# Fifteen loads of 1 to 15 partitions behind the 62nd tile of a nanmax

## The chip, the cores and the metric

The kernel runs on one core of one Trainium2 chip. The metric is the device time of one execution in microseconds (us). Four of the core's engines matter here: ScalarE (ACT), VectorE (DVE) and GpSimd (POOL), which compute, and SyncE (SP), which issues the DMAs. The transfers themselves run on 16 DMA engines.

## The reference

```
batch, seq, dim = 32, 2048, 2048
x = np.random.randn(batch, seq, dim).astype(np.float32)
x[np.random.rand(batch, seq, dim) < 0.1] = np.nan
np.nanmax(x, axis=-1).astype(np.float32)
```

It is a maximum over the last axis that passes over NaN: 65536 rows of 2048 float32 values go in (537 MB), 65536 values come out (0.26 MB).

## The kernel before

The rows are split over 128 partitions. A partition holds 512 rows, and a tile is a stretch of these, given in quarters of a row (`Q` = 512 values, 2 KB per partition). `TILES` lists the tiles in order; each has three lists in quarters: its loads, its pieces for the cleaning of NaN, and its reductions. Tile 1 has one load of 4 quarters. Tiles 2 to 62 have one load of 28 quarters each, which is 57344 bytes per partition and 7168 KB in all. From tile 63 on a tile has several loads, which get smaller towards the end (down to 1 quarter). `GROUPS` cuts the list into six groups; each has its own stretch of the input (`xg`) and of the output (`og`). The 62nd tile is the second of the fifth group.

There are three tile buffers `xt` (`BUFS`), so the load of tile 63 goes into the buffer of tile 60 and has to wait until DVE has reduced that one. A load (L316) is issued by SP, in program order. It waits for its buffer (`before`) and for the earlier load on its own lane: there are 14 lanes (`LANES`), one semaphore each, taken in turn.

For each piece ACT makes a key of the upper 16 bits of every value (L222, `kt<-xt`), and POOL turns the key back (L232, `xt<-kt`), so that NaN becomes a value that loses every comparison; a piece that is written with a minus sign is turned back by ACT instead. DVE takes the maximum of the cleaned rows (L239) into `acc`. At the end of some groups a short instruction corrects `acc` for rows without numbers (L245 on DVE; L260 and L274 on POOL for the fifth group).

The class `Order` keeps the order by hand. Its `add` issues an instruction, gives it the semaphore waits that its engine hasn't yet seen, directly or through another event, and lets it raise the semaphore of its lane. Only the last wait stands on the instruction; the others become instructions of their own in front of it (L158). Six stores of `acc` (L461), one for each group, come last on SP. Each waits for the event that makes its part of `acc` ready, and a last wait of SP holds the end of the program until they have landed.

Of the kernel before, what the change touches and what calls it, by code (L numbers as in the profile page):

```python
# [62 lines left out]
LEAD = 128  # L63

LANES = 14

# [104 lines left out]
def kernel(  # L173
# [15 lines left out]
    nc = tc.nc  # L189
    P = nc.NUM_PARTITIONS  # L190
    f32, i32 = mybir.dt.float32, mybir.dt.int32
# [14 lines left out]
    sing = ctx.enter_context(tc.tile_pool(name="sing", bufs=1))  # L206
# [4 lines left out]
    kts = [sing.tile([P, KEYS], u16, name=f"kt{i}") for i in range(NKEYS)]  # L211
    accs = sing.tile([P, sum(rows)], f32, name="acc")
    late = sing.tile([P, rows[LATE]], i32, name="late")

    with tc.tile_critical():  # L215
        order = Order(nc)
# [11 lines left out]
        def pool(deps, pair=None, **kw):  # L228
            return order.add(
                "pool",  # L230
                nc.gpsimd,
                lambda: nc.gpsimd.tensor_scalar(**kw),  # L232
                deps,
                lane=pair,
                joint=pair is not None,
            )

        def dve(deps, do, **kw):
            return order.add("dve", nc.vector, lambda: do(**kw), deps)  # L239

        def find(deps, acc):
            return order.add(
                "dve",
                nc.vector,
                lambda: nc.vector.scalar_tensor_tensor(  # L245
                    out=acc,
                    in0=acc,
                    scalar=LEAST,
                    in1=acc,
                    op0=ALU.is_ge,  # L250
                    op1=ALU.mult,
                ),
                deps,
            )
# [36 lines left out]
        number = 0  # L291
        lanes = [[] for _ in range(LANES)]
        turn = 0
        stores = []
        ready = []
        flagged = 0
        r0 = 0
        for gi, (s, g) in enumerate(zip(rows, GROUPS)):
            xg = xr[r0 : r0 + P * s].rearrange("(p s) d -> p (s d)", p=P)
# [5 lines left out]
            for loads, pieces, reds in g:  # L305
# [5 lines left out]
                for c in loads:  # L311
                    c *= Q
                    e = order.add(
                        "sp",
                        nc.sync,
                        lambda: nc.sync.dma_start(  # L316
                            out=xt[:, at : at + c], in_=xg[:, base + at : base + at + c]
                        ),
                        before + lanes[turn],
                        lane=f"load{turn}",  # L320
                        step=16,
                    )
                    lanes[turn] = [e]
                    turn = (turn + 1) % LANES
                    landed.append((at, at + c, e))
                    at += c
                clean = []
                after = []
                at = done = 0
# [24 lines left out]
                def name(i):  # L354
                    return f"pair{number}_{pairs[i][0]}" if i in pairs else None
# [15 lines left out]
                for parts in pieces:  # L371
# [4 lines left out]
                    if used + c > KEYS:  # L376
# [9 lines left out]
                        out=kts[key][:, used : used + c],  # L386
                        in_=xt[:, at : at + c].bitcast(i16)[:, 1::2],
# [6 lines left out]
                    for c in parts:  # L394
# [9 lines left out]
                        else:  # L404
                            e = pool(
                                [e_key],
                                name(piece),
                                out=to,
                                in0=kp,
                                scalar1=-1.0,  # L410
                                scalar2=float(TOP),
                                op0=ALU.mult,
                                op1=ALU.add,
# [4 lines left out]
                        while reds and done + reds[0] <= min([at] + open_):  # L418
                            n = reds.pop(0)
# [7 lines left out]
                            else:  # L427
                                m = max(n // D, 1)
                                to = acc[:, row : row + m]
                            e = dve(  # L430
                                [e for a, b, e in clean if b > lo and a < done] + part,
                                nc.vector.tensor_reduce,
                                out=to,
                                in_=xt[:, lo:done]
                                .bitcast(f32)
                                .rearrange("p (c d) -> p c d", c=m),
                                axis=mybir.AxisListType.X,
                                op=ALU.max,
# [13 lines left out]
            else:  # L452
                e = find(after, accs[:, lo:flagged])
# [3 lines left out]
        for (og, bits), e in zip(stores, ready):  # L457
            last = order.add(
                "sp",
                nc.sync,  # L460
                lambda: nc.sync.dma_start(out=og, in_=bits),  # L461
                [e],
                lane="store",
                step=16,
            )
# [38 lines left out]
```

## Time and profile before

| | |
|---|---|
| median of 3 runs | 1252.53 us (1252.52 to 1252.58) |
| profiled execution | 1252.48 us, of which the span is 1250.7 |
| POOL busy | 1168.5 us (93%), 242 instructions |
| DVE busy | 1111.4 us (89%), 179 instructions |
| ACT busy | 965.6 us (77%), 273 instructions |
| read from memory, written | 536.87 MB, 0.26 MB, 429 GB/s over the span |
| DMA packets | 15991, 2544 of them under 512 bytes |
| ACT's idle time before L222, ended by a load | 257.9 us in 69 waits |
| SP's waits for DVE before a load | 1155.4 us in 71 waits |
| tile loads of 7168 KB, issue to landing | 22.6 us (median of 61) |

The span runs from the first to the last recorded instruction; the time of an execution also holds what lies around it. In the profile, L316 is a line of the kernel, and "kt<-xt" says what an operation writes and reads, with the buffer numbers left out. A share of busy time is a mean over the whole span: which engine holds up the others has to be read from the waits at each place. DMA packets are the pieces that one DMA engine moves at a time: a load of 128 partitions is 128 packets, eight for each of the 16 engines, and on each engine a packet of 4 bytes follows, which raises the semaphore.

### The profile page before, as it was taken

What the parts mean: (1) busy time and instruction counts of PE and PEld (TensorE: products, weight loads), DVE (VectorE), ACT (ScalarE), POOL (GpSimd) and SP (SyncE); (2) the same over time, 40 slices, a digit from 0 to 9 for tenths busy, and PEclk for the clock granted to TensorE, in tenths of its full rate; (3) what the DMA queues carried; (4) which work ended last, traced back from release to release, by engine and by line L of the source; (5) the groups of instructions that cost most, each with busy time, mean ns of one, the idle gap of its engine ahead of it and who ended that gap; (6) DMA issues with size and microseconds to landing.
All of it is one profiled execution on the core that took longest, in us unless ns stands there. A gap on an engine that the chain in (4) does not pass through costs nothing.

```text
span 1250.7 us, 891 instructions
## 1 busy us (share of the span) xinstructions
DVE 1111.4 (89%) x179; ACT 965.6 (77%) x273; POOL 1168.5 (93%) x242
## 2 busy tenths in 40 slices
DVE  0888989888889888898988888998888899999999
ACT  3777887778777877788777877777777778999997
POOL 2999989998999899998999899999999999989998
DMA  9999999999999999999999999999999999999997
GB/s 415 440 418 433 440 440 438 413 440 440 440 433 418 440 440 438 429 424 440 440 436 424 431 440 438 436 424 433 440 438 435 422 436 436 425 434 429 431 428 301
DMA packets 15991, 537.20 MB, mean 430 GB/s; under 512 B 2544, under 2 KB 2544, under 8 KB 3568
## 3 DMA queue, kind: packets, MB, share of 16 engines
q1 hardware_dynamic: 15984, 537.14, 99.4%
q14 instruction: 7, 0.06, 0.0%
HBM read 536.87 MB, written 0.26 MB: 429 GB/s over the span
## 4 chain that ended last, share of the span: by engine, by line
DMA 40%; DVE 29%; POOL 22%; ACT 9%; issue 1%; SPq 0%
DMA xt<-in_x_dram 40%; DVE acc L239 29%; POOL xt L232 22%; ACT kt L222 8%; ACT xt L222 1%; SPq L316 0%; DVE acc L245 0%; SPq L499 0%; SPq L215 0%
## 5 line engine op out<-in xcount | busy, mean ns | idle before, releaser
L232 POOL TENSOR_SCALAR xt<-kt 128x3584 int16<-128x3584 uint16 (+11 forms) x236 | 1167.4, 4947 | 77.6 <-ACT kt L222 63.9
L239 DVE TENSOR_REDUCE acc<-xt 128x3 f32<-128x6144 f32 (+4 forms) x175 | 1107.5, 6379 | 135.6 <-POOL xt L232 128.1
L222 ACT ACTIVATE kt<-xt 128x3584 uint16<-128x3584 int16 (+9 forms) x247 | 913.4, 3734 | 278.0 <-DMA xt<-in_x_dram 257.9
L222 ACT ACTIVATE xt<-kt 128x512 int16<-128x512 uint16 (+6 forms) x24 | 52.8, 2202 | 0.7
L245 DVE SCALAR_TENSOR_TENSOR acc<-acc 128x414 f32<-128x414 f32 (+1 forms) x2 | 2.2, 1111 | 0.1
L222 ACT ACT_TABLE_LOAD x1 | 1.3, 1283 | 0.9 <-SPq L215 0.9
L239 DVE TENSOR_REDUCE xt<-xt 128x1 f32<-128x1536 f32 x1 | 1.7, 1743 | 0.0
L278 DVE MEMSET scalars<- 128x1 f32 x1 | 0.1, 59 | 1.0 <-SPq L215 1.0
L260 POOL TENSOR_SCALAR late<-acc 128x91 int32<-128x91 f32 x1 | 0.5, 549 | 0.1
L274 POOL TENSOR_TENSOR acc<-acc,late 128x91 int32<-128x91 int32 x1 | 0.3, 341 | 0.1
L485 POOL MEMSET const-float32-0.0<- 128x1 f32 x1 | 0.1, 98 | 0.2 <-issue 0.2
L222 ACT ACTIVATE scalars<-scalars 128x1 f32<-128x1 f32 x1 | 0.2, 203 | 0.0
L485 POOL MEMSET const-bfloat16-1.0<- 128x1 bf16 x1 | 0.1, 101 | 0.0
L485 POOL MEMSET const-uint8-127<- 128x1 uint8 x1 | 0.1, 101 | 0.0
L485 POOL MEMSET const-float32-1.0<- 128x1 f32 x1 | 0.1, 98 | 0.0
## 6 DMA issues: line engine op xcount, KB each, us to landing
xt<-in_x_dram SPq DMA_DIRECT2D x61, 7168.0 KB, 22.6
xt<-in_x_dram SPq DMA_DIRECT2D x2, 5120.0 KB, 17.4
xt<-in_x_dram SPq DMA_DIRECT2D x3, 2816.0 KB, 22.7
xt<-in_x_dram SPq DMA_DIRECT2D x4, 2048.0 KB, 22.3
xt<-in_x_dram SPq DMA_DIRECT2D x5, 1536.0 KB, 29.1
xt<-in_x_dram SPq DMA_DIRECT2D x2, 3584.0 KB, 24.8
xt<-in_x_dram SPq DMA_DIRECT2D x6, 1024.0 KB, 26.8
xt<-in_x_dram SPq DMA_DIRECT2D x3, 1792.0 KB, 30.1
```

Source lines behind the costliest of these rows:

```text
L222: lambda: nc.scalar.activation(**kw),
L232: lambda: nc.gpsimd.tensor_scalar(**kw),
L239: return order.add("dve", nc.vector, lambda: do(**kw), deps)
L245: lambda: nc.vector.scalar_tensor_tensor(out=acc, in0=acc, scalar=LEAST, in1=acc, op0=ALU.is_ge, op1=ALU.mult,),
L260: lambda: nc.gpsimd.tensor_scalar(out=none, in0=acc, scalar1=LEAST, scalar2=float(0x00400000), op0=ALU.is_lt, op1=ALU.mult,),
L274: lambda: nc.gpsimd.tensor_tensor(out=bits, in0=bits, in1=none, op=ALU.add),
L278: e_warm = order.add("dve", nc.vector, lambda: nc.vector.memset(warm, 1.0), [])
L485: nc = _bacc.Bacc("TRN2", target_bir_lowering=False, num_devices=1)
```

## The change

Right behind the load of the 62nd tile, SP issues fifteen more loads. Load n (1 to 15) copies the first 16 values, 64 bytes, of the group's stretch of the input on the first n partitions into its own 16 columns of a new tile, `spare`. They wait for nothing, and each raises a semaphore of its own, `run1` to `run15`. Nothing reads `spare`. The stores at the end wait for all fifteen, besides the event that they waited for before; after the first store has done so, SP has seen them.

```diff
+RUNS_BEHIND = 62
+RUNS = range(1, 16)
+SPARE = 16
...
     late = sing.tile([P, rows[LATE]], i32, name="late")
+    spare = sing.tile([P, len(RUNS) * SPARE], i32, name="spare")
...
         turn = 0
+        runs = []
         stores = []
...
                     landed.append((at, at + c, e))
                     at += c
+                if number == RUNS_BEHIND:
+                    for n in RUNS:
+                        runs.append(
+                            order.add(
+                                "sp",
+                                nc.sync,
+                                lambda: nc.sync.dma_start(
+                                    out=spare[:n, (n - 1) * SPARE : n * SPARE],
+                                    in_=xg[:n, :SPARE],
+                                ),
+                                [],
+                                lane=f"run{n}",
+                                step=16,
+                            )
+                        )
                 clean = []
...
                 nc.sync,
                 lambda: nc.sync.dma_start(out=og, in_=bits),
-                [e],
+                [e] + runs,
                 lane="store",
                 step=16,
```

## The prediction

> **What bounds the kernel now.** I read the page first, then the windows, then the last microseconds of ScalarE, then the queue of SP, and last the trace's records of single DMA packets.
>
> From the page: the span, the DMA row of the slices, the queues and the chain that ended last.
>
> ```profile
> span 1250.7 us, 891 instructions
> ...
> DMA  9999999999999999999999999999999999999997
> ...
> q1 hardware_dynamic: 15984, 537.14, 99.4%
> ...
> DMA xt<-in_x_dram 40%; DVE acc L239 29%; POOL xt L232 22%; ACT kt L222 8%; ACT xt L222 1%; SPq L316 0%; DVE acc L245 0%; SPq L499 0%; SPq L215 0%
> ```
>
> The 16 DMA engines are busy in every slice, and the load queue alone takes 99.4% of their span. The compute engines have idle time (POOL 93%, DVE 89%, ACT 77%), so the chain hops between engines, but what it comes back to is the transfer. By window:
>
> ```profile
> core 0: us, DVE busy (x) ACT busy (x) POOL busy (x), PEclk, DMA share, GB/s
> ...
> 1000.00:1100.00 100.00, 97.55 (x17) 84.29 (x23) 96.91 (x20) 1.00 1.00 432
> ...
> 1200.00:1242.00 42.00, 41.97 (x21) 39.50 (x29) 39.78 (x21) 1.00 1.00 420
> 1242.00:1250.70 8.70, 6.08 (x4) 3.17 (x5) 4.08 (x6) 1.00 0.05 10
> ```
>
> The share is 1.00 around the edit (the 62nd tile is issued at 1015.69) and stays 1.00 until 1242; only then do the engines run dry. In the packet records no two engines are idle at once between the first load and the last 1.3 us of transfers. So work added to a DMA engine behind tile 62 is not absorbed later. It goes to the end, unless that engine is one that waits for the others there. How directly the end hangs on the landing is seen in ScalarE's timeline:
>
> ```profile
> 1235.47 2.86 ACT L222 ACTIVATE kt<-xt 128x1536 uint16<-128x1536 int16 x2
> 1238.58 1.48 ACT L222 ACTIVATE kt<-xt 128x1536 uint16<-128x1536 int16 x1 [0.26 <-DMA xt<-in_x_dram]
> 1240.10 0.78 ACT L222 ACTIVATE xt<-kt 128x512 int16<-128x512 uint16 x1
> 1240.74 1.46 ACT L222 ACTIVATE kt<-xt 128x1536 uint16<-128x1536 int16 x1
> 1242.23 0.78 ACT L222 ACTIVATE xt<-kt 128x512 int16<-128x512 uint16 x1
> 1242.88 1.55 ACT L222 ACTIVATE kt<-xt 128x1024 uint16<-128x1024 int16 x2
> ```
>
> ACT waits 0.26 us for a load at 1238.58 and from there runs back to back; POOL, DVE (its last reduction at 1245.63) and the last store (1248.13) follow it. A later landing of that load moves the end by the same amount. An earlier one can bring 0.26 us, and then ACT is bound by its own work.
>
> A landing counts when the slowest of the 16 engines is through. The completion packets of tile 61's load begin, counted from the first, at 0, 38, 97, ... 494, 1017, 1158 and 1238 ns: thirteen engines lie within 0.5 us, three are late by 1.0 to 1.24 us. The spread at the last load is the same, with a fourth engine at 788. The three owe it to fetches of the instruction queue (8 KB, 309 ns): after each, that engine is 0.52 to 0.84 us later, and stays so. The end is therefore set by one engine with 1.24 us of lag, which does nothing but transfer.
>
> **The change part by part.**
>
> *Issue on SP.* Fifteen more DMA instructions stand behind the issue at 1015.69 and before that of tile 63 at 1032.58. The timeline of SP around them, and what it waited for from 1000 to 1040:
>
> ```profile
> 1015.69 0.33 SPq L316 DMA_DIRECT2D xt<-in_x_dram  x1
> 1032.58 0.80 SPq L316 DMA_DIRECT2D xt<-in_x_dram  x2
> SPq L316 <- DVE acc L239: 32.6, 2, 16.5
> ```
>
> SP has 16.5 us in between, waiting for DVE to free tile 63's buffer. A load that follows another costs 0.37 to 0.48 us in this trace, so fifteen cost 5.6 to 7.2 us: hidden. Without this cover they would delay tile 63's issue. That bites above 16.5/15 = 1.1 us each, and even then tile 62's load still runs to about 1037.7, some 5 us of queued work behind which a late issue hides. SP's issue blocks only when many descriptors stand in the queue: in the tail, with eight or nine loads ahead, single issues take 1.4 to 5.2 us. At 1016 there is one earlier load and tile 62's, about 13 packets for each engine; thirty more do not come near the 80 or so at which the tail blocks. Cost: 0.
>
> *The waits before the first store.* Fifteen semaphores, fourteen of them as instructions of their own at about 65 ns (the spacing of SP's waits after 1248.7), are 0.9 us ahead of the store at 1221.92. Behind it on SP stand only the other stores. The fifth is held by POOL's result:
>
> ```profile
> SPq L461 <- POOL acc L274: 15.5, 1, 15.5
> ```
>
> So 15.5 us of waiting take up the 0.9. The semaphores themselves were full 170 us before. Cost: 0.
>
> *The tile.* 960 bytes per partition that nobody reads; no address is shared. Cost: 0.
>
> *The packets.* This is what is left. The tiny loads stand in the rings behind tile 62's eight packets, before tile 63's. Their data are 1 + 2 + ... + 15 = 120 rows of 64 bytes, and each engine that takes part adds a completion packet per load. No row shows a 64-byte load. Nearest rows: 2048-byte load packets took 84 ns and 57344-byte ones 2116 ns, a line with 8.7 ns at zero and about 11 ns at 64 bytes; 28-byte store packets took 7 to 9 ns; a completion packet takes 9 ns and the next data packet starts 6 ns after it began. One tiny load therefore costs an engine 11 + 6 = 17 ns, call it 14 to 20. A window in the last store burst shows the same order:
>
> ```profile
> DMA packets 345, 0.18 MB, mean 308 GB/s; under 512 B 335, under 2 KB 335, under 8 KB 345
> ...
> q1 hardware_dynamic: 345, 0.18, 104.6%
> ```
>
> That is 0.6 us of 16 engines: 16 x 600 x 1.046 = 10042 ns, less ten 6144-byte packets at 234 ns, over 335 packets, 23 ns each at 4 to 420 bytes.
>
> How the rows spread over the engines no trace shows, since every DMA here has 128 partitions. Bounds: if the engine that is last gets none, 0. With an even spread each engine gets 7.5 rows and up to 15 completions, 7.5 x 11 + 15 x 6 = 0.17 us. With one row per engine and load, the engine hit most gets 15 x 17 = 0.26 us. With all 120 rows on the last engine, 120 x 11 + 15 x 6 = 1.41 us; on one of the thirteen early ones its lead of at least 0.74 us swallows half of that. I take one row per engine, and the late engine somewhere in the middle: about 0.15 us.
>
> The Trainium skill (DMA: Bandwidth & Descriptors, "Why a DMA increments its semaphore by 16 and not by 1") says that a DMA from SP runs on the largest number of engines, at most 16, that divides its slowest dimension, and on the lowest-numbered ones. By that, load n uses engines 0 to n-1 with one row each: engine 0 gets 15 packets and engine 15 none, a staircase of 17 ns a step, and the cost is 0 to 0.26 us depending on the number of the late engine. No run here shows it yet.
>
> Small packets may also break the stream. After each instruction fetch, the data packet in flight took 2333 to 2647 ns in place of 2116, so 217 to 531 ns longer. That was a switch of queue, which this is not; behind completion packets of the same queue I see no gap. I add a third of the smaller figure, 0.07 us, and keep the larger for the range.
>
> Sum: 0 + 0 + 0 + 0.15 + 0.07 = +0.22 us. The profiled execution took 1252.48 us (1250.7 of span, 1.8 around it), the median of the runs is 1252.53, so 1252.70 to 1252.75. I give 1252.75.
>
> **The rivals.**
>
> *Bubbles (1252.9 to 1255.0).* If 64-byte reads do not pipeline, each engine that takes part loses the 217 to 531 ns once, or the engine hit most loses more. For it: latency stands behind the first packets of the kernel, which took 0.5 to 0.85 us for 8 KB against 309 ns later. Against it: 2048-byte packets stream without a gap. Typical: +0.5 to +1.4 us, 1253.0 to 1253.9.
>
> *Serial completions (slower).* If a completion packet holds its engine until the data before it have been confirmed, the engine that carries all 15 pays 15 times. Above 2.5/15 = 0.167 us each (if that engine is the last; above 0.25 us if it is 1.24 us ahead) this is slower by over 0.2%. The four stores that end the queue put completions 175 ns apart on each engine with no gap, which bounds it at 15 x 0.175 = 2.6 us, 1255.2. That speaks for little more than that, but those are stores. At the 1.4 us that the last small stores need from issue to landing it would be 15 x 1.4 = 21 us, less the lead: about 1273.
>
> The Trainium skill (same page, "Anatomy of one DMA") puts a fixed cost of about 2 us on each DMA, mostly the receipt of the write. Taken as serial, it gives 15 x 2 = 30 us; the 175 ns spacing speaks against it.
>
> *A small gain (1252.3).* A fetch of instructions may fall elsewhere because SP's stream is 29 instructions longer. If the late engine loses one of its fetches, the end comes 0.26 us earlier at most, by ACT's wait. The two engines with the largest lags each had two fetches that came 692 and 745 us apart, 127 ScalarE and 128 POOL instructions; those streams do not change, so I give it little.
>
> *The change does nothing visible.* If the late engine gets no row, the time is 1252.53. It lies in the forecast.
>
> **How the numbers follow.** A measurement of this kernel tells about 0.2% from no change, 2.5 us: 1250.0 to 1255.0 counts as the same. Forecast with "nothing visible" (up to +0.35 us): 0.60. Bubbles: 0.22. Small gain: 0.06. Serial completions and whatever else costs over 2.5 us: 0.10. Faster by over 0.2%: 0.02, since every packet already takes its constant 2116 ns and the end gives back 0.26 us at most. So same is 0.60 + 0.22 + 0.06 = 0.88. The range runs from the small gain, 1252.3, to the bound by the stores' spacing, 1255.2; outside lie the dearer serial cases (0.07 or so) and the faster ones.
>
> **What would show it.** The load queue should hold between 135 and 360 packets more. SP's issue of tile 63 should stay 16.9 us behind tile 62's, with fifteen issues of some 0.4 us between. ACT's wait near 1238.6 should grow by what the span grows. The spread of tile 63's completions shows the spread over engines: the early engines move up by up to 0.26 us, the latest by less. I am wrong if tile 63's issue moves, if an engine stands still for over 1 us behind tile 62, or if the end moves by another amount than the latest engine does.

## The result and the profile after

The changed kernel takes 1254.29 us (median of 20 runs, 1254.07 to 1254.66) against 1252.52 (1252.32 to 1253.33): +1.77 us, a ratio of 1.0014 with an interval of 1.0007 to 1.002. It is slower by 0.14%, within the 0.2% called the same and inside the range, but eight times the forecast of +0.22 us. The profiled execution took 1254.30 us, of which the span is 1252.5.

The page of the changed kernel, the lines that answer to those of before:

```profile
span 1252.5 us, 913 instructions
...
DMA  9999999999999999999999999999999999999997
...
q1 hardware_dynamic: 16224, 537.15, 99.3%
...
DMA xt<-in_x_dram 41%; DVE acc L244 29%; POOL xt L237 19%; ACT kt L227 8%; ACT xt L227 1%; DVE acc L250 0%; SPq L322 0%; SPq L520 0%; SPq L220 0%
```

The load queue has 240 packets more, 120 rows and 120 completions: a load over n partitions raises its semaphore from n engines, one row each. The DMA engines are as full as before, and the span is 1.8 us longer. ScalarE's wait near the end moved by the same amount:

```profile
1240.37 1.48 ACT L227 ACTIVATE kt<-xt 128x1536 uint16<-128x1536 int16 x1 [0.28 <-DMA xt<-in_x_dram]
1241.89 0.77 ACT L227 ACTIVATE xt<-kt 128x512 int16<-128x512 uint16 x1
```

It starts at 1240.37 in place of 1238.58, and the work behind it follows at the same distances. The time was lost at the two loads of tile 63. Issue to landing of both (minimum, median, maximum), first before, then after:

```profile
DMA to landing us min/median/max: 17.5/19.8/22.0
```

```profile
DMA to landing us min/median/max: 19.3/21.6/23.8
```

Both land 1.8 us later after their issue. The issue itself did not move (SP's timeline and its waits, after):

```profile
1015.71 0.33 SPq L322 DMA_DIRECT2D xt<-in_x_dram  x1
1016.08 5.59 SPq L339 DMA_DIRECT2D spare<-in_x_dram  x15
1032.59 0.83 SPq L322 DMA_DIRECT2D xt<-in_x_dram  x2
...
SPq L322 <- DVE acc L244: 27.0, 2, 16.1
```

Fifteen issues take 5.59 us out of SP's wait. The loss lies in the 5 us in which the small packets pass, seen in the transfers from 1036.5 to 1041.5, before and after:

```profile
DMA packets 73, 2.42 MB, mean 483 GB/s; under 512 B 14, under 2 KB 14, under 8 KB 14
```

```profile
DMA packets 298, 2.10 MB, mean 419 GB/s; under 512 B 247, under 2 KB 247, under 8 KB 247
```

A packet counts here where it starts, which is why 483 lies above the 434 GB/s of longer stretches. 0.32 MB fewer start in these 5 us, though the small packets fill on average only some 0.1 us of an engine (120 x 13 ns over 16 engines).

The records of single packets show where the rest is. They don't name the DMA engine; a packet belongs to the engine whose last packet ended within a few ns of its start. A 64-byte packet took 11 ns and a tiny load 13 ns of its engine, packets back to back. Then the first 40960-byte packet of tile 63 comes, 1514 ns everywhere else. It took, by the number of tiny loads that the engine had just carried:

| tiny loads on the engine | 0 to 5 | 6 | 7 | 8 | 9 | 10 | 11 | 12 | 13 | 14 | 15 |
|---|---|---|---|---|---|---|---|---|---|---|---|
| over 1514 ns | 0 | 75 | 266 | 775 | 912 | 1062 | 1292 | 1220 | 1427 | 1585 | 1662 |

What a large packet takes over its usual time is called a stall here. From eight to fifteen loads it grows by 127 ns a load on average ((1662 - 775) / 7). The engine that was last (by 1.24 us) carried fourteen: 14 x 13 + 1585 = 1767 ns, which is the +1.77 us.

### The profile page after: what moved, and what is told of

It reads as the page before. It is cut to its first block, busy times and chain, and to the rows that moved or that the text cites. A ratio compares the mean times of both kernels' runs of the same rounds, so it can differ in the third digit from the quotient of the medians.

```text
span 1252.5 us, 913 instructions
## 1 busy us (share of the span) xinstructions
DVE 1111.7 (89%) x179; ACT 965.7 (77%) x273; POOL 1168.6 (93%) x242
## 3 DMA queue, kind: packets, MB, share of 16 engines
q1 hardware_dynamic: 16224, 537.15, 99.3%
## 4 chain that ended last, share of the span: by engine, by line
DMA 41%; DVE 29%; POOL 19%; ACT 10%; issue 1%; SPq 0%
DMA xt<-in_x_dram 41%; DVE acc L244 29%; POOL xt L237 19%; ACT kt L227 8%; ACT xt L227 1%; DVE acc L250 0%; SPq L322 0%; SPq L520 0%; SPq L220 0%
```

## The experiments

The theory to test: each DMA engine pays for its own small packets, 13 ns a load and a stall behind a long run of them; the end follows the engine that is last; and what makes the run stall is the completions, not the rows. All differences are medians against the kernel before on the same chip; single runs lie mostly within 0.3 us of their median, at most 0.8. The 95% intervals of these runs' ratios are 0.09% wide to either side, 1.1 us. So a difference under 1.1 us is not told from no change by them, and what is said of it rests on the packets in the traces as well.

**All fifteen loads on one engine.**

```diff
-                                    out=spare[:n, (n - 1) * SPARE : n * SPARE],
-                                    in_=xg[:n, :SPARE],
+                                    out=spare[:1, (n - 1) * SPARE : n * SPARE],
+                                    in_=xg[:1, :SPARE],
```

> Fifteen loads again, but each over one partition only. Theory (each engine's own queue pays, and the end follows the engine that is last): only one engine takes the fifteen rows and loses 15 x 13 ns plus 1.66 us on its next large packet, 1.86 us in all, as the engine with fifteen loads did in the changed kernel. It was 1.05 us ahead of the last engine there (0.19 against 1.24 us behind the first), so the end moves by about +0.8 us: 1253.3. Rival (a price per load, wherever it lands: 1.77/15 = 0.118 us each): +1.77 us, 1254.3. Rival (one late engine costs nothing): 1252.5.

+0.80 us (1253.58 against 1252.78). One engine carries 31 small packets between tiles 62 and 63, the other fifteen only their completion of tile 62; that engine's next packet is 1646 ns too long, all others take 1514. In this trace it was 0.41 us behind the first engine and the last one 1.49: 0.41 + 0.19 + 1.65 - 1.49 = 0.76. So the price is paid on one engine, and its lead over the last one is subtracted.

**Three runs of five.**

```diff
-                if number == RUNS_BEHIND:
-                    for n in RUNS:
+                if RUNS_BEHIND - 2 <= number <= RUNS_BEHIND:
+                    for n in RUNS[RUNS_BEHIND - number :: 3]:
```

> The same fifteen loads, five each behind tiles 60, 61 and 62 (3, 6, 9, 12, 15; 2, 5, 8, 11, 14; 1, 4, 7, 10, 13), so that no engine gets more than five in a row. Theory (the stall comes from a long run of small packets in one queue, none up to five loads): only the packets' own time is left on the engine that was last, 14 x 13 ns = +0.18 us: 1252.7. Rival (each small load costs its engine the same, alone or in a run: 1.77/14 = 0.126 us): +1.77 us, 1254.3.

+0.52 us (1253.30 against 1252.78), between the two. The packets behind a run of five were 18 to 192 ns too long. Cutting the run takes most of the price away, but five are not free, as the zeros of the table suggested.

**One load behind each of fifteen tiles.**

```diff
-                if number == RUNS_BEHIND:
-                    for n in RUNS:
+                if RUNS_BEHIND - 15 < number <= RUNS_BEHIND:
+                    for n in [RUNS_BEHIND + 1 - number]:
```

> The same fifteen loads, one behind each of tiles 48 to 62 (15 partitions first, 1 last), so completions never stand in a row. Theory (completions pile up): only the packets' time is left, 14 x 13 ns, +0.2 us over before. If a part of the stall is paid for each load whatever stands behind it, as three runs of five suggest (+0.52 us, of which 0.18 are packets, so 0.024 us a load): +0.5 us. If all of it is: +1.8 us.

+0.28 us (1253.05 against 1252.77). No stall shows behind the single loads: but for those that follow an instruction fetch, no large packet from tile 48 on is over 6 ns too long. ScalarE's last wait, in a profiled execution of 1253.37 us, the slowest of the eleven:

```profile
1239.43 1.48 ACT L227 ACTIVATE kt<-xt 128x1536 uint16<-128x1536 int16 x1 [0.24 <-DMA xt<-in_x_dram]
```

The same fifteen loads, the same rows and semaphores, cost 0.28 us apart and 1.77 in a row. What costs most is that they stand in a row.

**Rows in halves.**

```diff
-                                    in_=xg[:n, :SPARE],
+                                    in_=xg[:n, : 2 * SPARE].rearrange("p (c d) -> p c d", c=2)[
+                                        :, :, : SPARE // 2
+                                    ],
```

(`out` is cut in two in the same way.)

> The same fifteen loads, each row in two pieces of 32 bytes that do not lie together, so each engine gets two data packets and one completion per load: the completions are as many as in the changed kernel, the reads twice as many. If completions stall the queue: the stall stays at 1.6 us on the last engine and only the packets' time grows by some 14 x 10 ns, +1.9 us, 1254.4. If small reads stall it: 28 reads on the last engine in place of 14; at the 0.13 us per read by which the stall grew from eight to fifteen loads, +1.8 us more, +3.6 us in all, 1256.1.

+2.07 us (1254.85 against 1252.78). Twice the rows add 0.3 us and not 1.8. On three of the late engines the last packet of tile 62, ahead of the small ones, was 64 to 66 ns too long, which the changed kernel doesn't show.

**One load of fifteen pieces.**

```diff
-RUNS = range(1, 16)
+RUNS = range(15, 16)
...
+                                    out=spare[:16, :].rearrange("p (c d) -> p c d", c=15),
+                                    in_=xg[:16, : 30 * SPARE].rearrange("p (c d) -> p c d", c=15)[
+                                        :, :, :SPARE
+                                    ],
```

> One load over 16 partitions in place of fifteen, with fifteen separate pieces of 64 bytes per partition: every engine gets fifteen small reads and one completion. If completions stall the queue: one completion cannot, and only 15 x 11 ns of packets are left, +0.2 us, 1252.7. If small reads stall it: every engine stalls as the one with fifteen loads did, 1.66 us, with 0.2 us of packets: +1.8 us, 1254.4. If it is the count of all small packets, 16 here: as with eight loads, 0.78 + 0.15 us, +0.9 us, 1253.4.

+0.30 us (1253.08 against 1252.78). Every engine reads fifteen rows and completes once; the next packets are 4 to 92 ns too long. On the last engine tile 62's last packet was 100 ns too long, the small packets took 115 ns and the next packet was 92 too long: 0.31 us. Fifteen rows of 64 bytes in a row do not stall an engine by more than that.

**Eight loads on all engines.**

```diff
-RUNS = range(1, 16)
+RUNS = range(1, 9)
...
-                                    out=spare[:n, (n - 1) * SPARE : n * SPARE],
-                                    in_=xg[:n, :SPARE],
+                                    out=spare[:16, (n - 1) * SPARE : n * SPARE],
+                                    in_=xg[:16, :SPARE],
```

> Eight loads over 16 partitions each, so every engine, the last one too, gets eight loads in a row. By the changed kernel's trace the engine with eight loads lost 8 x 13 ns and a stall of 0.78 us: +0.9 us over before. If the stall had to do with the unequal lengths of the runs (an engine that waits for another): +0.1 us.

+0.87 us (1253.53 against 1252.66), as worked out from the table. The stalls are 310 to 831 ns, the three late engines' 613 to 706. Beside the single load of fifteen pieces this is the plainest pair: 16 small packets on every engine in both, 8 rows with 8 completions stall it by half a microsecond and more, 15 rows with one completion hardly at all. A completion comes here with a load of its own, which SP issues on its own; no run parts the two, so it is not shown whether the completion packet or the separate load is what costs.

**Another source, other addresses, one semaphore.** Three runs each change one thing that a completion might wait for. From SBUF:

```diff
+    near = sing.tile([P, SPARE], i32, name="near")
...
+        e_near = order.add("dve", nc.vector, lambda: nc.vector.memset(near, 0), [])
...
-                                    in_=xg[:n, :SPARE],
+                                    in_=near[:n, :],
...
-                                [],
+                                [e_near],
```

> The same fifteen loads, but their rows are read from a small tile of SBUF that VectorE sets to zero at the start, not from the input. If the completions stall the queue by themselves, wherever the data come from: +1.8 us over before, as the change. If the stall is the time that a 64-byte read of device memory takes to come back before its completion may go: it goes, and +0.2 us of packets is left.

From columns 8 KB apart (`in_=xg[:n, n * D : n * D + SPARE]`):

> The same fifteen loads, each from columns of its own, 8 KB apart, where the changed kernel reads the same 64 bytes of a row up to fifteen times. If repeated reads of one address cause the stall: +0.2 us over before. If the completions do: +1.8 us.

With `lane="run"` for all fifteen:

> The change as it is, but all fifteen loads raise one semaphore, for whose full count the first store waits. If the number of semaphores matters (their waits on SP, or completions to different places): less than +1.4 us over before. If only the number of completions does: +1.8 us.

+1.94 us (1254.71 against 1252.77), +1.71 (1254.48 against 1252.77) and +1.87 (1254.53 against 1252.66). None takes the stall away: it is not the time of a read of device memory, not repeated reads of one address, and not the number of semaphores. The first of them changes a little more than its text says: its load over one partition ran as sixteen pieces of 4 bytes, one on each engine (30 packets more in the load queue, 16254 against 16224), so each engine but one carried one load more, and each issue took 0.62 to 0.79 us. At 13 + 127 ns for that load, +1.91 us would be expected.

**Behind tile 20.** `RUNS_BEHIND = 20`.

> The change as it is, but behind tile 20. If the lag of an engine is never made good, since the DMA engines do not idle until the last loads: +1.8 us over before, as behind tile 62. If 43 tiles give the engine time to catch up: 0 to +0.3 us.

+1.88 us (1254.54 against 1252.66). Forty-two more tiles give no engine time to catch up. The changed kernel's trace shows the same: the last engine is 2.81 us behind the first at 1065 and still at 1145.

**Completions further apart.** Two runs were meant to show whether completions are worked off at a pace of their own.

```diff
-                                    in_=xg[:n, :SPARE],
+                                    in_=xg[:n, : 2 * SPARE].rearrange("p (c d) -> p c d", c=8)[
+                                        :, :, : SPARE // 8
+                                    ],
```

(`out` is cut in eight.)

> The same fifteen loads, each row in eight pieces of 8 bytes that do not lie together, so completions come some 60 ns apart on an engine in place of 13. If completions are worked off at a pace of their own, about 0.13 us each, and the packets' time counts against that: 0.87 us of packets (14 x 62 ns) and 0.9 us of stall, +1.8 us over before. If the stall is added whatever the spacing: 0.87 + 1.6, +2.5 us. If small reads add their own stall: over +2.7 us.

+3.02 us (1255.79 against 1252.77), in number the third expectation, but here the issue on SP changed too. SP's timeline, and the transfers from 1036 to 1041.5 in 40 slices:

```profile
1015.88 0.33 SPq L322 DMA_DIRECT2D xt<-in_x_dram  x1
1016.25 21.15 SPq L339 DMA_DIRECT2D spare<-in_x_dram  x15
1037.45 2.09 SPq L322 DMA_DIRECT2D xt<-in_x_dram  x2
```

```profile
DMA  0000126536502133110011112399990009000000
GB/s 0 0 0 0 2 4 8 7 5 62 0 2 3 1 3 5 1 2 0 0 2 3 3 3 2 1 894 1489 1192 596 0 0 0 596 0 0 0 0 0 0
```

The engine hit most would have 135 packets of the small loads queued, and the issue blocked: the ninth of the fifteen, with 72 packets of small loads ahead of it on that engine, took 3.1 us and the eleventh 12.3. Tile 63's load left 4.9 us late (1037.45 against 1032.59); its first large packets started at 1039.70 to 1040.61 in place of 1036.57 to 1037.87, and fewer than half of the engines were busy for 2.2 us. But a late engine, which had small packets to move nearly all of that time, lost as much without it: tile 62's last packet was 840 ns too long, the small packets took 0.99 us and the next packet was 1247 ns too long, 3.1 us in all. It finished that packet 23 ns before the last engine did. So two losses of one size stand side by side, and the run says nothing about the pace. The second try stayed under the queue that blocks the small loads:

```diff
-RUNS = range(1, 16)
+RUNS = range(1, 9)
...
+                                    out=spare[:16, (n - 1) * SPARE : n * SPARE - 2].rearrange(
+                                        "p (c d) -> p c d", c=7
+                                    ),
+                                    in_=xg[:16, : 28].rearrange("p (c d) -> p c d", c=7)[
+                                        :, :, :2
+                                    ],
```

> As the kernel with eight loads over 16 partitions, each row in seven pieces of 8 bytes: the completions stand some 55 ns apart on an engine in place of 13, and the queue holds 77 packets at most, short of where SP's issue blocks. If completions are worked off at a pace of their own and packets between them take part of that time: 0.44 us of packets and a stall shorter by 0.34 us, +0.9 us over before, as with whole rows. If the stall is added whatever the spacing: +1.2 us.

+2.40 us (1255.06 against 1252.66): both expectations fail. The first packets of tile 63 were 997 to 1607 ns too long, and the last packets of tile 62 on the three late engines 579 to 851 ns, although those stand ahead of their own small packets. On the very last engine that is 851 + 377 of small packets + 1007 = 2.24 us. The issues of the eight small loads took 0.43 us each; the second load of tile 63 took 2.08, where it takes 0.43 in the changed kernel, but its packets come only behind twelve us of the first load's. So the theory, completions and not rows, doesn't hold as it stands: rows do count where there are many of them, at least 8-byte rows between completions. That engines then hold each other up is a guess from the packets ahead. How rows and completions share the stall, and what an engine waits for in it, stays open.

## Why the prediction came out as it did

**Issue on SP: right.** Fifteen issues were put at 5.6 to 7.2 us; they took 5.59, and tile 63 was issued 16.88 us behind tile 62. Named as the limit was a queue of some 80 packets; 43 were safe, and the run of eighths blocked near that number, on its way to 135.

**Waits before the first store: right at 0, with a wrong count.** SP took two semaphores per instruction: seven instructions, 0.46 us. They went into its wait for POOL, 15.7 us long:

```profile
SPq L482 <- POOL acc L279: 15.7, 1, 15.7
```

**Time of the packets: right.** 17 ns a load were expected, 13 measured; 0.15 us on the last engine, 0.18 measured, though this engine was not in the middle but carried fourteen of the fifteen. The staircase that follows from the Trainium skill's rule (DMA: Bandwidth & Descriptors, "Why a DMA increments its semaphore by 16 and not by 1") is there: the engines carry 0, 1, ... 15 loads, and fifteen loads of one partition all go to one engine. That these are the lowest-numbered engines can't be seen, since the records don't name them. The late engines, those that fetch instructions, carry 11 to 14.

**Bubbles: the term that was mis-sized.** The sum took 0.07 us, and the last engine lost 1.59. The step that failed was "behind completion packets of the same queue I see no gap", carried from completions at least 0.6 us apart on an engine (loads) and 175 ns apart (stores, with no large packet behind them) to completions 13 ns apart. Single ones cost next to nothing in the runs either; eight in a row do. That the time lies in the range is owed to the rivals, which set its upper end; the sum itself was too small by a factor of eight. The rival "bubbles" held the time (1252.9 to 1255.0) but priced it as one loss of 0.22 to 0.53 us for an engine, where it grows with the run; its typical +0.5 to +1.4 us stop short of +1.77, and its reason, 64-byte reads that do not pipeline, is not what the runs show: fifteen reads with one completion cost 0.30 us. A sign of being wrong that the prediction named, an engine that stands still for over 1 us behind tile 62, came true in substance: six engines lost over 1 us there, as a longer packet and not as a gap between packets.

**Serial completions: not seen as worded, and bounded by luck.** No completion packet held its engine: each took 9 ns, and the loss stands in the next large packet. The bound of 15 x 0.175 = 2.6 us held, but with rows in sevenths eight completions cost 2.40 us, where it would be 1.4. The growth is 0.127 us a load, under the 0.167 from which it would have passed 0.2%. The Trainium skill (same page, "Anatomy of one DMA") gives its fixed cost of about 2 us for a DMA that GpSimd issues. Taken for each of these loads, which SP issues, and paid one after another, it would be 15 x 2 = 30 us; the measured +1.77 us refutes that.

**How the end follows: right.** The last engine's landing moved the end one to one within the scatter (1.77 us worked out and measured), through ScalarE's wait, from tile 62 and from tile 20 alike, and an engine that leads has its lead subtracted.

**The gain by another fetch: not seen.** One instruction fetch did move (from 1129.9 to 1026.0), on an engine that is not the last.

## What to carry to other kernels

Where the DMA engines never idle, as here, an engine that falls behind stays behind, and the end waits for the slowest of the sixteen: ask of every added transfer which engines carry it, and which of these is last already. Keep tiny transfers apart from each other or make one of them: fifteen in a row cost 1.77 us, fifteen apart 0.28, one with fifteen pieces 0.30. Making the pieces much smaller is no way out: eight loads of 8-byte pieces cost 2.40. A price seen for a packet on its own is no price for a row of them; look for a row in the trace that has the same spacing, and take the larger bound where there is none.

## What was not expected of the hardware

- A 40960-byte packet took 3176 ns in place of 1514 behind fifteen completed 64-byte loads. With rows from SBUF the longest took 3260 (1.94 against 1.77 us in all).
- 56 reads of 8 bytes on each engine, with eight completions, also stretched the large packets ahead of them on the late engines by 0.58 to 0.85 us.
- Each 8 KB instruction fetch delays its DMA engine by over half a microsecond (0.52 to 0.84), and the engines hit stay late to the end: four engines had all the fetches from 248 to 1130 us, and in the changed kernel the four late engines are those that carry 11 to 14 of the fifteen loads.
